# The fourth group of w_down by seven products, and the final norm in another order of columns

## The chip, the cores and the metric

One core of one Trainium2 chip. The metric is the device time of one execution in microseconds (us), lower is better; before the change it was 947.31 us, the median of three runs (946.19 to 949.31).

## The reference, cut to what matters

The kernel is one layer of an encoder on 512 tokens of width 1024, in fp32. The change touches only its end:

```python
hn = rmsnorm(h, norm_mlp)
h = h + square(relu(hn @ w_up)) @ w_down     # w_up 1024x4096, w_down 4096x1024
out = rmsnorm(h, norm_final)                 # rows scaled by (mean of squares + 1e-6)**-0.5
```

## The kernel before, in words

**Precision.** Each fp32 product is made of three fp32r matmuls. An operand `src` is split into a high part (a copy rounded to fp32r, on ACT, line 96) and a low part (`src` less the high part, on DVE, line 103). TensorE (PE) then adds high x high, low x high and high x low in PSUM.

**The stage w_up, w_down.** The 4096 hidden features go in four groups `g` of 1024. `up_unit(g, m)` makes 128 hidden features for all 512 tokens (24 matmuls of 512 columns, a relu and a square on ACT into `R[g, m // 4]`). Groups 0, 1 and 2 of w_down are multiplied in Strassen-Winograd form: hidden features and output columns are halved, tokens too, and seven products of a 256-token by 512-feature operand "A" with a 512x512 operand "B" take the place of eight. Each is 24 matmuls: `product(g, x)`, x from 0 to 6. The A operands are blocks of `R` or their sums `S1` to `S4` (`a_sum`, on DVE or POOL) and are split by `a_split`; the B operands are blocks of w_down or their sums `T1` to `T4` (`b_sum`, on POOL, 128x1024 each, T2, T3, T4 written over a block), two halves `q` each. Group 3 is multiplied plainly: `tokmajor` for output columns 0 to 511, then `tok_inner` for each of the four blocks `t` of 128 tokens for columns 512 to 1023, the last block in two halves of 256 columns.

**Sums.** A product ends in PSUM, and `add_to` adds it to `h_t` on DVE. The PSUM tile of products 2, 4 and 6 is one chain ("b"), that of 3 and 5 another ("c"). Product 0 of each group has a tile of its own and goes into an SBUF sum `X1` (`add_x1`); `x1_out` adds X1 to all eight parts of `h_t` on POOL during group 3.

**What sets the order.** It is written by hand. A tick is three matmuls; `later(n, f)` issues f n ticks on, and each engine works through its own instructions in the order of issue, as soon as what they read is there. `plan(g)` (line 1391) puts the sums and A splits of a group at ticks. The pieces of weights (and B halves) stand in one list; `use(i)` (line 235) issues the splits of piece i + 2, its high part one tick on, its low part two. Three buffers of each part go round (line 197), so that the split of a piece waits until the piece three before it has been multiplied. Between product x and x + 1 of a group stands `up_unit(g + 1, x)`, and two of them (6 and 7) end the group. A unit lasts eight ticks, as a product does, and uses one piece where a product uses two.

**The end.** The last norm takes blocks of 128 tokens in turn: squares of columns 0 to 511 early, then `add_h`, squares of the rest (ACT), a scale and a power of one column (POOL), and one `stt` of 128x1024 on DVE that writes `hn`, from which the block is stored. The last block's halves each end with an add (DVE) and squares (ACT), in PSUM tiles of their own:

```python
for q in range(2):
    p = ps()
    ...
    tt(h[:, hc], p[:, c], h[:, hc], ADD)
```

Of the kernel before, what the change touches and what calls it, by code (L numbers as in the profile page):

```python
# [9 lines left out]
F32 = mybir.dt.float32  # L10
# [8 lines left out]
L = 512  # L19
# [36 lines left out]
def trunk(ctx: ExitStack, tc: tile.TileContext, a: dict, out):  # L56
# [7 lines left out]
    def fr(t):  # L64
        return t.bitcast(F32)
# [14 lines left out]
    def zr():  # L80
        return z(F32R)
# [20 lines left out]
    def tt(o, i, j, op, eng=None):  # L102
        (eng or VE).tensor_tensor(out=o, in0=i, in1=j, op=op)  # L103
# [150 lines left out]
    def rows(w, k0, nk, c0, n=512):  # L254
        return w[k0 * 128:(k0 + nk) * 128, c0:c0 + n].rearrange("(k p) f -> p k f", p=128)
# [26 lines left out]
    DN = ("11", "21", "T2", "T1", "T3", "22", "T4")  # L282
    Bt = {}
    P_up = [[] for _ in range(4)]
    P_st, P_dn3 = [], [[], []]

    def add_up(g, m):
        P_up[g].append(add_piece(cols(w_up, 1024 * g + 128 * m)))

    for m in range(8):  # L290
        add_up(0, m)
    for g in range(3):
        P_st.append([])
        for x, nm in enumerate(DN):
            P_st[g].append([add_piece(lambda g=g, nm=nm, q=q: Bt[g, nm, q], "s") for q in range(2)])
            add_up(g + 1, x)
        add_up(g + 1, 7)
# [1037 lines left out]
    X1 = [mlp_p.tile([128, 512], F32, name=f"X{t}") for t in range(2)]  # L1335

    R, A_hl, S_t = {}, {}, {}
    T0, T1 = slice(0, 256), slice(256, 512)
# [14 lines left out]

    AN = ("A11", "A12", "S2", "S1", "S3", "S4", "A22")

    def a_split(g, x):
        def hi():
            src = a_block(g, x) if AN[x][0] == "A" else S_t[g, AN[x]]
            h = str_p.tile([128, 4, 256], F32R, tag="ah", name="ah", bufs=3)
            copy(SE, h, src)  # L1360
            A_hl[g, x] = (src, h)

        def lo():
            src, h = A_hl[g, x]
            l = str_p.tile([128, 4, 256], F32R, tag="al", name="al", bufs=3)
            tt(l, src, fr(h), SUB)
# [20 lines left out]
    def b_t1(g):  # L1387
        for q in range(2):
            later(4 * q, lambda q=q: b_sum(g, "T1", q, "12", "11", SUB))

    def plan(g):

        ra, rb = R[g, 0], R[g, 1]
        at = lambda n, *fs: [later(n + i, f) for i, f in enumerate(fs)]
        S = lambda nm: (lambda: S_t[g, nm])
        at(4, *a_split(g, 1))
        at(6, lambda: a_sum(g, "S1", lambda: ra[:, :, T1], lambda: rb[:, :, T1], ADD, VE))
        at(8, lambda: a_sum(g, "S2", S("S1"), lambda: ra[:, :, T0], SUB, VE))
        at(18, *a_split(g, 2))
        at(22, lambda: a_sum(g, "S4", lambda: rb[:, :, T0], S("S2"), SUB, GE))  # L1400
        for n, x in ((34, 3), (50, 4), (66, 5), (82, 6)):
            at(n, *a_split(g, x))
# [15 lines left out]
    def add_x1(g, t, p):
        if g == 0:
            copy(SE, X1[t], p)  # L1420
        else:
            tt(X1[t], p, X1[t], ADD)

    chain = {}

    CH = (("a", None), ("d", (0, 0)), ("b", (0, 1)), ("c", (1, 1)), ("b", (1, 1)), ("c", (0, 1)), ("b", (1, 0)))

    def product(g, x):
# [4 lines left out]
        acc = chain[g, nm]  # L1433
        for q in range(2):
            hs, ls = use(P_st[g][x][q])
            ah, al = A_hl[g, x]
            for i in range(2):
                k = 2 * q + i
                for t in range(2):
                    o = slice(128 * t, 128 * t + 128)  # L1440
                    st, sp = first and k == 0, k == 3
                    kw = {} if first else {"skip_group_check": True}
                    TE.matmul(acc[t], ah[:, k, o], hs[i], start=st, stop=False, **kw)  # L1443
                    TE.matmul(acc[t], al[:, k, o], hs[i], start=False, stop=False, **kw)  # L1444
                    TE.matmul(acc[t], ah[:, k, o], ls[i], start=False, stop=sp, **kw)  # L1445
                    tick()
        for t in range(2):
            if to is None:
                later(1 + t, lambda t=t: add_x1(g, t, acc[t]))
            else:  # L1450
                later(1 + t, lambda t=t: add_to(2 * to[0] + t, to[1], acc[t]))


    us = []
# [22 lines left out]
    aT_h, aT_l = [], []

    def a3(m):
        h, l = zr(), zr()  # L1480
        aT_h.append(h)
        aT_l.append(l)
        r = R[3, m // 4][:, m % 4]
        copy(SE, h, r)
        tt(l, r, fr(h), SUB)

    def x1_out(t, hf):
        o = h_t[t][:, 512 * hf:512 * hf + 512]
        tt(o, X1[t % 2], o, ADD, GE)

    for g in range(3):
        plan(g)
        for x in range(7):
            product(g, x)
            up_unit(g + 1, x)
        if g == 2:

            str_p.release()
            z_p = tc.alloc_tile_pool(name="z2", bufs=36, reuse_waits="tile")
            for m in range(4):  # L1500
                later(2 * m, lambda m=m: a3(m))
        up_unit(g + 1, 7)
    for m in range(4, 8):
        later(2 * m - 7, lambda m=m: a3(m))
    for n in range(8):
        later(2 + 2 * n, lambda n=n: x1_out(n // 2, n % 2))
    add_all(0, tokmajor(P_dn3[0], aT_h, aT_l))
    for t in range(3):
        p = tok_inner(P_dn3[1], aT_h, aT_l, t)
        o = hn_tile()  # L1510
        first_squares(t, o)
        add_h(t, 1, p)
        norm_rows(t, g_fin, o)
# [4 lines left out]
    first_squares(t, o)
    hg = xT_p.tile([128, 8, L], F32, tag="h", name="hg").rearrange("p a b -> p (a b)")[:, 0:1024]

    g32 = hg[:, 768:1024]
    ts(g32, g_fin[:, 768:1024], 32.0, 1.0, MUL, MUL, GE)
    stt(hg[:, 0:512], h[:, 0:512], 32.0, g_fin[:, 0:512], MUL, MUL)
    s2 = sm(2)
    for q in range(2):
        p = ps()
        c, hc = slice(256 * q, 256 * q + 256), slice(512 + 256 * q, 768 + 256 * q)
        for k in range(8):
            hs, ls = splits[P_dn3[1][k // 2]]
            mm3(p[:, c], aT_h[k][:, tok], aT_l[k][:, tok], hs[k % 2][:, c], ls[k % 2][:, c], k == 0, k == 7)  # L1530
        tt(h[:, hc], p[:, c], h[:, hc], ADD)
        SE.activation(out=o[:, hc], in_=h[:, hc], func=AF.Square, accum_out=s2[:, q:q + 1])
        if q == 0:
            tt(ss_t[t], ss_t[t], s2[:, 0:1], ADD, GE)
            stt(hg[:, hc], h[:, hc], 32.0, g_fin[:, hc], MUL, MUL)
    rs = sm()
    tt(rs, s2[:, 1:2], ss_t[t], ADD, GE)
    tt(rs, rs, mhalf, ALU.pow, GE)
    stt(o[:, 768:1024], h[:, 768:1024], rs, g32, MUL, MUL)
    SE.activation(out=o[:, 0:512], in_=hg[:, 0:512], func=AF.Copy, scale=rs)  # L1540
    SP.dma_start(out=out[tok, 768:1024], in_=o[:, 768:1024])
    SP.dma_start(out=out[tok, 0:512], in_=o[:, 0:512])
    ts(o[:, 512:768], hg[:, 512:768], rs, 1.0, MUL, MUL)
    SP.dma_start(out=out[tok, 512:768], in_=o[:, 512:768])
# [73 lines left out]
```

## Time and profile before

| | us |
|---|---|
| median of three runs | 947.31 |
| the profiled execution's own time | 945.39 |
| its span (first to last instruction) | 943.5 |
| PE busy | 920.4 |
| DVE busy | 589.6 |
| ACT busy | 446.3 |
| POOL busy | 342.7 |

All sections of the trace count from the start of the span. PE's records overlap each other, since matmuls are pipelined: the distance from one start to the next says what a matmul costs, not the length of its record. The low parts on DVE, the sums on POOL and the adds all have line 103, as they go through one helper; they are told apart by the names of their tiles.

### The profile page before, as it was taken

To read this page: it belongs to the slowest core of one execution; us is meant where nothing else is said; L and a number is where in the kernel's file an instruction comes from. 1 tells how busy PE (TensorE), PEld (TensorE's weight loads), DVE (VectorE), ACT (ScalarE), POOL (GpSimd) and SP (SyncE) were. 2 spreads that over 40 slices of the span, in tenths; PEclk is the share of its full clock that TensorE was granted. 3 is DMA by queue.
4 is the path that set the end of the run, shared out by engine and by line. 5 is a ranking of instruction groups with operands and counts; after the bars stand their busy time and mean duration, and the time that the engine had idled before them with its cause. 6 is when DMAs were issued, how large, how long until landed. Compare 5 with 4: busy or idle time off the path is not lost.

```text
span 943.5 us, 12801 instructions
## 1 busy us (share of the span) xinstructions
PE 920.4 (98%) x4683; PEld 739.0 (78%) x4683; DVE 589.6 (62%) x897; ACT 446.3 (47%) x711; POOL 342.7 (36%) x440
## 2 busy tenths in 40 slices
PE   9899989999999999998999999999999999999997
PEld 6788767777767888886888888888888888888876
DVE  4688778886653765668374554436665857775443
ACT  5634656656754334455343343346444444444522
POOL 0600246555788886233110000146134314511302
PEclk9999989999999999999999999999999999999998
DMA  9237666542312335354512255272333124221222
GB/s 315 87 116 197 166 166 178 167 136 85 103 48 78 90 90 138 82 139 130 159 47 89 90 170 186 68 250 62 94 112 130 49 94 148 90 67 45 67 90 90
DMA packets 140462, 111.05 MB, mean 118 GB/s; under 512 B 16368, under 2 KB 117104, under 8 KB 140400
## 3 DMA queue, kind: packets, MB, share of 16 engines
q1 hardware_dynamic: 140400, 110.24, 39.3%
q8 instruction: 37, 0.61, 0.3%
q14 instruction: 25, 0.20, 0.1%
HBM read 106.32 MB, written 3.90 MB: 117 GB/s over the span
## 4 chain that ended last, share of the span: by engine, by line
PE 87%; DVE 6%; ACT 2%; issue 2%; DMA 2%; POOL 1%; SPq 0%; POOLq 0%; DVEq 0%; ACTq 0%
PE ps L122 22%; PE ps L121 22%; PE ps L123 22%; PE ps L1444 4%; PE ps L1445 4%; PE ps L1443 4%; PE ps L810 3%; PE ps L794 2%; DVE z L103 1%; ACT z L96 1%; PE ps L1124 1%; PE ps L764 1%; PE ps L763 1%; DVE S L767 1%; DVE wl L103 1%
## 5 line engine op out<-in xcount | busy, mean ns | idle before, releaser
L103 DVE TENSOR_TENSOR wl<-raw,wh 128x1024 fp32r<-128x1024 f32 (+1 forms) x113 | 159.6, 1414 | 169.8 <-ACT wh L96 169.0
L121 PE MATMUL ps<-xh,wh 128*128 128x512 f32 x384 | 156.6, 408 | 0.0
L123 PE MATMUL ps<-xh,wl 128*128 128x512 f32 x384 | 150.7, 393 | 2.9 <-DVE wl L103 2.9
L122 PE MATMUL ps<-xl,wh 128*128 128x512 f32 x384 | 150.2, 391 | 0.0
L96 ACT ACTIVATE wh<-raw 128x1024 fp32r<-128x1024 f32 (+1 forms) x112 | 117.5, 1049 | 35.3 <-PE ps L123 7.9
L96 ACT ACTIVATE z<-ps 128x512 f32<-128x512 f32 (+4 forms) x128 | 72.9, 578 | 65.1 <-PE ps L123 24.2
L122 PE MATMUL ps<-hl,wh 128*128 128x512 f32 (+1 forms) x272 | 102.5, 377 | 0.3 <-DVE hl L103 0.3
L121 PE MATMUL ps<-hh,wh 128*128 128x512 f32 (+1 forms) x272 | 102.5, 377 | 0.2 <-ACT hh L96 0.2
L123 PE MATMUL ps<-hh,wl 128*128 128x512 f32 (+1 forms) x272 | 102.5, 377 | 0.0
L123 PEld LDWEIGHTS ps<-xh,wl 128*128 128x128 f32 x384 | 72.3, 188 | 19.1 <-DVE wl L103 3.3
L109 POOL TENSOR_SCALAR S<-S,sm 128x512 f32<-128x512 f32 x64 | 58.5, 930 | 79.1 <-DMA z<-Ud 58.7
L121 PEld LDWEIGHTS ps<-xh,wh 128*128 128x128 f32 x384 | 72.7, 189 | 14.2 <-PE ps L810 0.8
L122 PEld LDWEIGHTS ps<-xl,wh 128*128 128x128 f32 x384 | 72.8, 190 | 12.9
L1344 ACT ACTIVATE R<-ps 128x512 f32<-128x512 f32 x32 | 19.1, 598 | 128.2 <-PE ps L123 128.2
L103 POOL TENSOR_TENSOR z<-z 128x512 f32<-128x512 f32 x24 | 39.4, 1661 | 92.8 <-DVE z L106 42.2
L774 ACT ACTIVATE S<-S,sm 128x512 f32<-128x512 f32 x64 | 46.2, 722 | 56.1 <-DVE sm L109 52.7
L1443 PE MATMUL ps<-wh,ah 128*128 128x512 f32 x168 | 65.4, 389 | 0.0
L1444 PE MATMUL ps<-wh,al 128*128 128x512 f32 x168 | 65.4, 389 | 0.0
L1445 PE MATMUL ps<-wl,ah 128*128 128x512 f32 x168 | 65.4, 389 | 0.0
L109 POOL TENSOR_SCALAR sm<-sm 128x1 f32<-128x1 f32 (+1 forms) x16 | 3.6, 223 | 163.0 <-ACT hn L1314 137.7
L103 DVE TENSOR_TENSOR z<-z 128x512 f32<-128x512 f32 (+1 forms) x68 | 55.7, 824 | 10.5 <-ACT z L96 7.0
L103 POOL TENSOR_TENSOR B<-B,B 128x1024 f32<-128x1024 f32 x18 | 51.3, 2865 | 28.8 <-DVE wl L103 14.0
(209 smaller groups left out, 1931.3 us busy)
## 6 DMA issues: line engine op xcount, KB each, us to landing
raw<-in_w_in_dram SPq DMA_DIRECT2D x55, 512.0 KB
raw<-in_w_up_dram SPq DMA_DIRECT2D x32, 512.0 KB
B<-in_w_down_dram SPq DMA_DIRECT2D x24, 512.0 KB
T<-in_ttab_dram SPq DMA_DIRECT2D x16, 448.0 KB
z<-Fd SPq DMA_DIRECT2D x16, 256.0 KB
raw<-in_w_branch_attn_dram SPq DMA_DIRECT2D x8, 512.0 KB
raw<-in_w_out_dram SPq DMA_DIRECT2D x8, 512.0 KB
raw<-in_w_down_dram SPq DMA_DIRECT2D x8, 512.0 KB
```

The costliest lines, as they stand in the source:

```text
L96: SE.activation(out=o, in_=i, func=AF.Copy, scale=scale)
L103: (eng or VE).tensor_tensor(out=o, in0=i, in1=j, op=op)
L109: (eng or VE).tensor_scalar(out=o, in0=i, scalar1=s1, scalar2=s2, op0=op0, op1=op1)
L121: TE.matmul(o, wh, xh, start=first, stop=False)
L122: TE.matmul(o, wh, xl, start=False, stop=False)
L123: TE.matmul(o, wl, xh, start=False, stop=last)
L774: SE.activation(out=s, in_=s, func=AF.Exp, bias=nm, accum_out=den[h][:, t:t + 1])
L810: TE.matmul(p[64 * b:64 * b + 64], vt[kt][h // 8][:, c:c + 64], pts.pop((h, kt)), start=kt == 0, stop=kt == 3)
L1344: SE.activation(out=r, in_=p, func=AF.Relu)
L1443: TE.matmul(acc[t], ah[:, k, o], hs[i], start=st, stop=False, **kw)
L1444: TE.matmul(acc[t], al[:, k, o], hs[i], start=False, stop=False, **kw)
L1445: TE.matmul(acc[t], ah[:, k, o], ls[i], start=False, stop=sp, **kw)
```

## The change

Group 3 of w_down is multiplied by seven products as well. Product 0 starts chain "b", is added to block (0, 0) and goes on under product 2; `X1`, `add_x1`, `x1_out` and `a3` go. The pieces are listed in one order with the products, and in group 2 the units of group 3 stand earlier: after products 4 and 5 two each, and none after product 6. In group 3 nothing stands between the products; its plan has other ticks, and the low parts of its A operands 3 to 6 go to POOL. The last norm takes the left columns of blocks 2 and 3 last, and `end` is product 6 of group 3 with that norm: `one(q, i, t, c)` issues three matmuls into `acc[t][:, c]` and a tick. What follows the last add is as before, with left and right columns changed over.

```diff
-    for x in range(8):
-        i, hf = x // 2, x % 2
-        P_dn3[hf].append(add_piece(rows(w_down, 24 + 2 * i, 2, 512 * hf), "wz"[hf]))
+    ORDER = []
+    for g in range(4):
+        for x in range(7):
+            ORDER.append(("p", g, x))
+            if g < 2:
+                ORDER += [("u", g + 1, x)] + [("u", g + 1, 7)] * (x == 6)
+            elif g == 2:
+                ORDER += [("u", 3, m) for m in ((0,), (1,), (2,), (3,), (4, 5), (6, 7), ())[x]]
...
+        last = g == 3
+        at(0 if last else 4, *a_split(g, 1))
+        at(1 if last else 6, lambda: a_sum(g, "S1", lambda: ra[:, :, T1], lambda: rb[:, :, T1], ADD, VE))
+        at(2 if last else 8, lambda: a_sum(g, "S2", S("S1"), lambda: ra[:, :, T0], SUB, VE))
+        at(4 if last else 18, *a_split(g, 2))
+        at(5 if last else 22, lambda: a_sum(g, "S4", lambda: rb[:, :, T0], S("S2"), SUB, GE))
+        for n, x in (((12, 3), (19, 4), (27, 5), (35, 6)) if last else ((34, 3), (50, 4), (66, 5), (82, 6))):
+            at(n, *a_split(g, x, GE if last else None))
         for q in range(2):
+            if not last:
+                at(2 + 4 * q, lambda q=q: b_sum(g, "T3", q, "22", "12", SUB))
+            at((4 + 2 * q) if last else (12 + 4 * q), lambda q=q: b_sum(g, "T2", q, "T3", "11", ADD))
+            at((20 + 3 * q) if last else (36 + 4 * q), lambda q=q: b_sum(g, "T4", q, "21", "T2", SUB))
+        if g < 3:
+            e = 8 * (g == 2)
...
-    CH = (("a", None), ("d", (0, 0)), ("b", (0, 1)), ...
+    CH = (("b", (0, 0)), ("d", (0, 0)), ("b", (0, 1)), ...
...
+    def norm_out(t, c, scale, eps):
+        o = o_t[t]
+        s2 = sm()
+        SE.activation(out=o[:, c], in_=h_t[t][:, c], func=AF.Square, accum_out=s2)
+        rs = sm()
+        ts(s2, s2, ss_t[t], scale, ADD, MUL, GE)
+        tt(rs, s2, mhalf, ALU.pow, GE)
+        stt(o, h_t[t], rs, g_fin, MUL, MUL)
         SP.dma_start(out=out[t * 128:t * 128 + 128, :], in_=o)
...
+    def end(one, acc):
+        for q in range(2):
+            for i in range(2):
+                one(q, i, 0)
+        add_to(2, 0, acc[0])
+        norm_out(2, lo, 1.0 / D, EPS)
...
+        stt(hg[:, 512:1024], h[:, 512:1024], 32.0, g_fin[:, 512:1024], MUL, MUL)
+        for n in range(2):
+            c = slice(256 * n, 256 * n + 256)
+            for q in range(2):
+                for i in range(2):
+                    one(q, i, 1, c)
+            tt(h[:, c], acc[1][:, c], h[:, c], ADD)
+            SE.activation(out=o[:, c], in_=h[:, c], func=AF.Square, accum_out=s2[:, n:n + 1])
...
+        if g == 3 and x == 5:
+            for t in range(2):
+                later(3 + t, lambda t=t: norm_out(t, slice(512, 1024), 1.0 / D, EPS))
```

## Rows read from the trace of the kernel before

**Rows 1.** The page: busy time by engine, and the chain that ended last.
```profile
PE 920.4 (98%) x4683; PEld 739.0 (78%) x4683; DVE 589.6 (62%) x897; ACT 446.3 (47%) x711; POOL 342.7 (36%) x440
...
PE 87%; DVE 6%; ACT 2%; issue 2%; DMA 2%; POOL 1%; SPq 0%; POOLq 0%; DVEq 0%; ACTq 0%
```

**Rows 2.** Waits of PE, 560 to 945 us: waiting, releaser, us, times, longest.
```profile
PE ps L122 <- DVE wl L103: 1.4, 1, 1.4
```

**Rows 3.** Timeline of PE, 884 to 945 us: start, us, engine, line, operation, [idle].
```profile
890.80 0.39 PE L121 MATMUL ps<-wh,z 128*128 128x512 f32 x1
...
896.24 0.39 PE L121 MATMUL ps<-wh,z 128*128 128x512 f32 x1
898.07 0.50 PE L122 MATMUL ps<-wl,z 128*128 128x512 f32 x1 [1.44 <-DVE wl L103]
...
930.38 0.39 PE L123 MATMUL ps<-z 128*128 128x512 f32 x1
930.61 0.28 PE L121 MATMUL ps<-z 128*128 128x256 f32 x1
...
936.24 0.28 PE L123 MATMUL ps<-z 128*128 128x256 f32 x1
```

**Rows 4.** Groups by line and form, 560 to 945 us: busy us, mean ns.
```profile
L96 ACT ACTIVATE wh<-B 128x1024 fp32r<-128x1024 f32 x36 | 37.9, 1052 | 17.2 <-PE ps L1444 10.3 <-issue 5.8 <-POOL T L103 1.2
...
L103 DVE TENSOR_TENSOR h<-ps,h 128x512 f32<-128x512 f32 x51 | 33.1, 682 | 13.8 <-PE ps L123 13.8
...
L103 POOL TENSOR_TENSOR S<-R 128x1024 f32<-128x1024 f32 x3 | 7.2, 2401 | 77.6 <-ACT R L1345 55.1 <-DMA B<-in_w_down_dram 22.5
```

**Rows 5.** Timeline of POOL, 817 to 827 us.
```profile
817.56 2.40 POOL L103 TENSOR_TENSOR S<-R,S 128x1024 f32<-128x1024 f32 x1 [7.07 <-DVE S L103]
819.91 6.75 POOL L103 TENSOR_TENSOR B<-B,B 128x1024 f32<-128x1024 f32 x2
```

**Rows 6.** Timeline of DVE over the same stretch.
```profile
816.19 1.22 DVE L103 TENSOR_TENSOR S<-S,R 128x1024 f32<-128x1024 f32 x1
817.33 1.28 DVE L103 TENSOR_TENSOR X<-ps,X 128x512 f32<-128x512 f32 x2
818.53 2.51 DVE L103 TENSOR_TENSOR wl<-B,wh 128x1024 fp32r<-128x1024 f32 x1
822.53 1.87 DVE L103 TENSOR_TENSOR wl<-raw,wh 128x1024 fp32r<-128x1024 f32 x1 [1.49 <-ACT wh L96]
824.32 3.42 DVE L103 TENSOR_TENSOR al<-S,ah 128x1024 fp32r<-128x1024 f32 x1
```

**Rows 7.** Timeline of ACT after the last unit of group 3.
```profile
885.56 0.60 ACT L1344 ACTIVATE R<-ps 128x512 f32<-128x512 f32 x1 [7.33 <-PE ps L123]
886.19 0.63 ACT L1345 ACTIVATE R<-R 128x512 f32<-128x512 f32 x1
```

**Rows 8.** Timeline of PE, 40 to 49 us: before and after an idle stretch.
```profile
44.30 0.79 PE L122 MATMUL ps<-wl,z 128*128 128x512 f32 x1 [2.39 <-DVE wl L103]
...
45.32 0.63 PE L121 MATMUL ps<-wh,z 128*128 128x512 f32 x1
...
47.46 0.51 PE L123 MATMUL ps<-wh,z 128*128 128x512 f32 x1
47.80 0.39 PE L121 MATMUL ps<-wh,z 128*128 128x512 f32 x1
```

**Rows 9.** Timeline of DVE at the end.
```profile
930.81 0.69 DVE L103 TENSOR_TENSOR h<-ps,h 128x512 f32<-128x512 f32 x1 [1.61 <-PE ps L123]
933.36 1.28 DVE L106 SCALAR_TENSOR_TENSOR hn<-h,sm,g 128x1024 f32<-128x1024 f32 x1 [1.86 <-POOL sm L103]
934.56 0.88 DVE L106 SCALAR_TENSOR_TENSOR hg<-h,g 128x512 f32<-128x512 f32 x1
935.37 0.41 DVE L103 TENSOR_TENSOR h<-ps,h 128x256 f32<-128x256 f32 x1
...
936.56 0.42 DVE L103 TENSOR_TENSOR h<-ps,h 128x256 f32<-128x256 f32 x1 [0.32 <-PE ps L123]
```

More of the change, by code (lines that the diff above doesn't have):

```diff
@@ L284, in trunk @@
     P_up = [[] for _ in range(4)]
-    P_st, P_dn3 = [], [[], []]
+    P_st = [[] for _ in range(4)]
     def add_up(g, m):
         P_up[g].append(add_piece(cols(w_up, 1024 * g + 128 * m)))
+    ORDER = []
[6 more added lines that the diff above has]
+                ORDER += [("u", 3, m) for m in ((0,), (1,), (2,), (3,), (4, 5), (6, 7), ())[x]]
     for m in range(8):
         add_up(0, m)
-    for g in range(3):
-        P_st.append([])
-        for x, nm in enumerate(DN):
-            P_st[g].append([add_piece(lambda g=g, nm=nm, q=q: Bt[g, nm, q], "s") for q in range(2)])
-            add_up(g + 1, x)
-        add_up(g + 1, 7)
-    for x in range(8):
-        i, hf = x // 2, x % 2
-        P_dn3[hf].append(add_piece(rows(w_down, 24 + 2 * i, 2, 512 * hf), "wz"[hf]))
+    for kind, g, x in ORDER:
+        if kind == "u":
+            add_up(g, x)
+        else:
+            nm = DN[x]
+            P_st[g].append([add_piece(lambda g=g, nm=nm, q=q: Bt[g, nm, q], "s") for q in range(2)])
     ident = const.tile([128, 128], F32, name="ident")
@@ L1334, in trunk @@
     str_p = tc.alloc_tile_pool(name="strassen", bufs=1, reuse_waits="tile")
-    X1 = [mlp_p.tile([128, 512], F32, name=f"X{t}") for t in range(2)]
     R, A_hl, S_t = {}, {}, {}
@@ L1354, in trunk, with a_split @@
     AN = ("A11", "A12", "S2", "S1", "S3", "S4", "A22")
-    def a_split(g, x):
+    def a_split(g, x, eng=None):
         def hi():
@@ L1365, in lo @@
             l = str_p.tile([128, 4, 256], F32R, tag="al", name="al", bufs=3)
-            tt(l, src, fr(h), SUB)
+            tt(l, src, fr(h), SUB, eng)
             A_hl[g, x] = (h, l)
@@ L1395, in plan @@
         S = lambda nm: (lambda: S_t[g, nm])
[L1396 to L1402, printed above, removed]
-        for q in range(2):
-            at(2 + 4 * q, lambda q=q: b_sum(g, "T3", q, "22", "12", SUB))
-            at(12 + 4 * q, lambda q=q: b_sum(g, "T2", q, "T3", "11", ADD))
-            at(36 + 4 * q, lambda q=q: b_sum(g, "T4", q, "21", "T2", SUB))
@@ L1407, in plan @@
-        if g < 2:
+        last = g == 3
[6 more added lines that the diff above has]
+            at(n, *a_split(g, x, GE if last else None))
@@ L1408, in plan @@
+        for q in range(2):
+            if not last:
[4 more added lines that the diff above has]
+            e = 8 * (g == 2)
             for n, nm in ((44, "11"), (76, "12"), (92, "22"), (108, "21")):
                 at(n, lambda nm=nm: b_load(g + 1, nm))
-            at(112, lambda: b_t1(g + 1))
@@ L1411, in plan @@
-            at(98, lambda: a_sum(g + 1, "S3", lambda: R[g + 1, 0][:, :, T0], lambda: R[g + 1, 0][:, :, T1], SUB, GE))
-            at(104, *a_split(g + 1, 0))
+            at(112 - e, lambda: b_t1(g + 1))
+            if g == 2:
+                for q in range(2):
+                    at(113 + 3 * q, lambda q=q: b_sum(3, "T3", q, "22", "12", SUB))
+            at(98 - e, lambda: a_sum(g + 1, "S3", lambda: R[g + 1, 0][:, :, T0], lambda: R[g + 1, 0][:, :, T1], SUB, GE))
+            at(104 - e, *a_split(g + 1, 0))
@@ L1416, in add_to, with product @@
         tt(o, p, o, ADD)
[L1418 to L1422, printed above, removed]
     chain = {}
-    CH = (("a", None), ("d", (0, 0)), ("b", (0, 1)), ("c", (1, 1)), ("b", (1, 1)), ("c", (0, 1)), ("b", (1, 0)))
-    def product(g, x):
+    CH = (("b", (0, 0)), ("d", (0, 0)), ("b", (0, 1)), ("c", (1, 1)), ("b", (1, 1)), ("c", (0, 1)), ("b", (1, 0)))
+    def product(g, x, end=None):
         nm, to = CH[x]
@@ L1433, in product, with one @@
         acc = chain[g, nm]
+        def one(q, i, t, c=slice(0, 512), last=None):
+            hs, ls = splits[P_st[g][x][q]]
+            ah, al = A_hl[g, x]
+            k = 2 * q + i
+            o = slice(128 * t, 128 * t + 128)
+            st = first and k == 0
+            kw = {} if first else {"skip_group_check": True}
+            TE.matmul(acc[t][:, c], ah[:, k, o], hs[i][:, c], start=st, stop=False, **kw)
+            TE.matmul(acc[t][:, c], al[:, k, o], hs[i][:, c], start=False, stop=False, **kw)
+            TE.matmul(acc[t][:, c], ah[:, k, o], ls[i][:, c], start=False, stop=k == 3, **kw)
+            tick()
+        if end:
+            for q in range(2):
+                use(P_st[g][x][q])
+            end(one, acc)
+            return
         for q in range(2):
-            hs, ls = use(P_st[g][x][q])
-            ah, al = A_hl[g, x]
+            use(P_st[g][x][q])
             for i in range(2):
-                k = 2 * q + i
                 for t in range(2):
[L1440 to L1446, printed above, removed]
+                    one(q, i, t)
         for t in range(2):
[L1448 to L1451, printed above, removed]
+            later(1 + t, lambda t=t: add_to(2 * to[0] + t, to[1], acc[t]))
     us = []
@@ L1476, in trunk @@
         up_unit(0, m)
[L1477 to L1513, printed above, removed]
-        SP.dma_start(out=out[t * 128:t * 128 + 128, :], in_=o)
-    t, h, o = 3, h_t[3], hn_tile()
-    tok = slice(384, 512)
@@ L1518, in trunk @@
[L1518 to L1544, printed above, removed]
+    o_t = {}
+    def half_squares(t, hf):
+        o_t[t] = hn_tile() if t < 2 else raw()
+        ss_t[t] = sm()
+        c = slice(512 * hf, 512 * hf + 512)
+        SE.activation(out=o_t[t][:, c], in_=h_t[t][:, c], func=AF.Square, accum_out=ss_t[t])
@@ new lines, in norm_out, with ss_eps, early @@
+    def norm_out(t, c, scale, eps):
[6 more added lines that the diff above has]
+        stt(o, h_t[t], rs, g_fin, MUL, MUL)
+        SP.dma_start(out=out[t * 128:t * 128 + 128, :], in_=o)
+    def ss_eps(t):
+        ts(ss_t[t], ss_t[t], 1.0, D * EPS, MUL, ADD, GE)
+    def early(t, hf):
+        half_squares(t, hf)
+        ss_eps(t)
@@ new lines, in end @@
+    def end(one, acc):
+        lo = slice(0, 512)
+        for q in range(2):
+            for i in range(2):
+                one(q, i, 0)
+        add_to(2, 0, acc[0])
+        norm_out(2, lo, 1.0 / D, EPS)
+        h, o = h_t[3], o_t[3]
+        hg = xT_p.tile([128, 8, L], F32, tag="h", name="hg").rearrange("p a b -> p (a b)")[:, 0:1024]
+        g32 = hg[:, 256:512]
+        ts(g32, g_fin[:, 256:512], 32.0, 1.0, MUL, MUL, GE)
+        stt(hg[:, 512:1024], h[:, 512:1024], 32.0, g_fin[:, 512:1024], MUL, MUL)
+        s2 = sm(2)
+        for n in range(2):
+            c = slice(256 * n, 256 * n + 256)
+            for q in range(2):
+                for i in range(2):
+                    one(q, i, 1, c)
+            tt(h[:, c], acc[1][:, c], h[:, c], ADD)
+            SE.activation(out=o[:, c], in_=h[:, c], func=AF.Square, accum_out=s2[:, n:n + 1])
+            if n == 0:
+                tt(ss_t[3], ss_t[3], s2[:, 0:1], ADD, GE)
+                stt(hg[:, c], h[:, c], 32.0, g_fin[:, c], MUL, MUL)
+        rs = sm()
+        tt(rs, s2[:, 1:2], ss_t[3], ADD, GE)
+        tt(rs, rs, mhalf, ALU.pow, GE)
+        tok = slice(384, 512)
+        stt(o[:, 256:512], h[:, 256:512], rs, g32, MUL, MUL)
+        SE.activation(out=o[:, 512:1024], in_=hg[:, 512:1024], func=AF.Copy, scale=rs)
+        SP.dma_start(out=out[tok, 256:512], in_=o[:, 256:512])
+        SP.dma_start(out=out[tok, 512:1024], in_=o[:, 512:1024])
+        ts(o[:, 0:256], hg[:, 0:256], rs, 1.0, MUL, MUL)
+        SP.dma_start(out=out[tok, 0:256], in_=o[:, 0:256])
@@ new lines, in trunk @@
+    for kind, g, x in ORDER:
+        if kind == "u":
+            up_unit(g, x)
+            continue
+        if x == 0:
+            plan(g)
+        product(g, x, end if (g, x) == (3, 6) else None)
+        if g == 3 and x == 1:
+            for t in range(2):
+                later(4 + 2 * t, lambda t=t: early(t, 0))
+        if g == 3 and x == 4:
+            for t in range(2):
+                later(4 + t, lambda t=t: early(2 + t, 1))
+        if g == 3 and x == 5:
+            for t in range(2):
+                later(3 + t, lambda t=t: norm_out(t, slice(512, 1024), 1.0 / D, EPS))
@@ L1545, in trunk @@
+    str_p.release()
     h_p.release()
-    z_p.release()
     mlp_p.release()
```

## The prediction

> **What bounds the kernel now.** I read the page first: PE is busy for 98% of the span and makes 87% of the chain that ended last [rows 1]. So a microsecond is gained by taking matmuls away, as long as PE is not made to wait. Then the waits of PE for the end of the kernel: from 560 to 945 us only one exceeds 0.3, of 1.4 us, for a low part on DVE, in the plain multiplication of group 3 [rows 2, 3]. All else in the stage is hidden behind PE. Then PE's timeline for what a matmul costs. Between the starts 890.80 and 896.24 lie 24 steps, 0.2267 us each for 512 columns; the 48 matmuls of 256 columns from 930.61 to 936.24 take 0.12 us each [rows 3]. The records' own lengths (0.39) overlap and would say almost twice as much. A tick is thus 0.68 us and a product 5.44 us. Last I read DVE and POOL side by side where both are at work [rows 5, 6], since the change moves work to POOL and takes away the units between which DVE had time.
>
> What is to be seen there: the sum S4 on POOL takes 2.40 us from 817.56, undisturbed. The low part on DVE that starts at 818.53 takes 2.51 instead of 1.22, the time of a sum of its size at 816.19: it stands still until POOL ends at 819.96, and runs 1.08 from then. POOL's next pair takes 6.75 instead of 4.8, and DVE's two low parts beside it 1.87 and 3.42. All six instructions fit one rule, the two engines take turns by whole instructions: POOL holds for about 2.28 (from DVE's end at 824.39 to its own at 826.66), DVE for 1.08, and who comes second waits. Only the adds out of PSUM (X, two in 1.28) run through unhindered.
>
> **The change part by part.** I call G the moment when group 3's first matmul of w_down starts (890.80 now), and count from it. Up to G the amount of matmuls is the same; the order of units in group 2 changes, but nothing waits there now and each split still has 5.4 us, so 0 (at most the 1.4 us that the one wait cost).
>
> *Removed matmuls.* Now: 168 of 512 columns and 48 of 256, 38.1 + 5.8 = 43.9 us, and with the wait for DVE 45.6 (890.80 to 936.36). After: seven products of 24, the last one with 12 of its matmuls cut into 24 halves: 156 x 0.2267 + 24 x 0.12 = 38.2 us. The gain is 7.3 us: 5.6 of matmuls and 1.7 of the wait with its restart. X1's adds are replaced by as many adds to h (0), the eight `x1_out` on POOL and the splits of single hidden blocks go (hidden, 0), and eight loads of w_down become eight loads of the same 512 KB, issued on SP before G with nothing behind them but stores (0).
>
> *The feed of group 3.* A half product (2.72 us) needs one split: a high part on ACT, 1.05 [rows 4], and a low part on DVE, 1.22. It can start only when the piece three before is done, so 5.44 us before use. On DVE each product adds two adds of 0.68 [rows 4]; without POOL this is 3.8 us of 5.44 and fits. But POOL now has nine instructions of 2.40 in the same 33 us (T2 and T4 in two halves each, S4, four low parts of A), each holding DVE up for as much as 2.28. By hand, in DVE's order of issue:
> - The last unit ends at G-5.4; relu and square of it occupy ACT until G-4.1 [rows 7]; then come high and low part of product 0's two halves, until G-0.4. POOL's T2, first half, has waited for the second low part and holds until G+1.8.
> - DVE: an add (0.2), the low part of A12, which waits for POOL, G+1.8 to 2.9; S1 to 4.0; an add; S2 to 5.8; the low part of product 1's first half to G+6.9. PE wants it at G+5.9: it waits **1.1 us**.
> - S4 on POOL has waited since S2 and holds from G+6.9 to 9.2. The low part of S2 on DVE comes next, to 10.3; then T2's second half on POOL, to 12.6; then the low part of product 1's second half, to G+13.7. PE wants it at 9.8: **3.9 us**.
> - The clock: after an idle of 2.39 us PE went on at 0.43 us a matmul, the level of 1.2 GHz, for eight matmuls or so, 44.30 to 47.80 [rows 8], while an idle of 1.44 left it at 0.23 [rows 3]. The wait of 3.9 should do the same: eight times 0.2 and the restarts, **2.0 us**.
> - After that PE is late enough that DVE and POOL, in turns, keep ahead of it.
>
> Sum: product 6 starts at G + 32.66 (144 matmuls) + 7.0 = G+39.6. The low end of this term is 0, if DVE and POOL do not hinder each other there; the high end takes one more hold of 2.28 with its clock, 10.5.
>
> *The end.* Now the last 48 halves (5.8 us) cover the norm of block 2. After the change, DVE has in its queue behind product 5: the low part of the last piece, two adds, two `stt` of blocks 0 and 1, the add of block 2, its `stt`, the `stt` for hg, and only then the two adds of the last halves. Each `stt` of 1.28 waits for squares on ACT and two small steps on POOL: from the start of an add to the start of its `stt` 2.55 us (930.81 to 933.36), and what stands behind waits too [rows 9]. From product 6's start: the first add at 1.8, `stt` at 4.3 and 5.5, add of block 2 at 6.7, its `stt` at 9.2, hg at 10.4 (0.8), first half's add 11.2 to 11.6. PE has finished the first half at 4.2.
> The second half of the matmuls now goes to the other columns of the tile that this add reads; before, each half had a tile of its own, and ran through at 0.12 [rows 3]. No row shows one part of a PSUM tile read while another is written. I bound it by 0 (PE runs on at once; the second add then follows the hg `stt` at 12.0) and by a full wait: PE starts at 11.7 after 7 idle us, 12 halves at the slow level [rows 8], 0.24 each, and the second add starts at 14.9. I take the wait, as a write after a read of the same tile, and keep 2.9 us less for the range.
> The Trainium skill ("PSUM — Partial Sum Buffer", section "PSUM bank collisions raise a hardware error") says that TensorE writing and VectorE reading one bank and quadrant raise an error even at disjoint columns, and that PSUM is to be guarded by bank, not by address. By that rule the wait must be there; no run here shows it yet.
> From the second add to the span's end it is 943.5 - 936.56 = 6.94, unchanged: same steps, columns changed over.
>
> *Sum.* Now G to the second add: 45.8. After: 39.6 + 14.9 = 54.5. So +8.8 us, against the profiled execution's 945.39 (span 943.5 and 1.9 around it), which is 954.2. The median of the runs lies 1.9 above that execution, so for it 947.3 + 8.8 = **956.1 us**.
>
> **The rivals.**
> *No wait for the shared PSUM tile.* Only the end differs: the second add at 12.0, so +5.9 and 953.2. For it: the columns are disjoint. Against it: the tile is one.
> *DVE and POOL do not hinder each other* (the other side). Then group 3 has no wait and product 6 starts at G+32.7. The crowded end stays, as it waits for small steps and not for a shared resource: 10 to 12.6 us to the second add (the first add no longer stands behind a late low part, and starts at -0.5 instead of 1.8). That gives -3.3 without the tile's wait, 944.0, and -0.5 with it, 946.9. It decides by whether the low part of product 1's second half ends by G+9.8. For it: DVE and POOL each have less than 5.44 us a product on their own numbers. Against it: all the instructions of [rows 5, 6] but X.
> *Group 3 waits more than the hand chain says.* Low parts of 3.4 us as at 824.32 [rows 6] for products 3 to 5 exceed the 2.72 of a half; if one more wait goes to PE with its clock, +3.5: 959.6.
> That the change does not save the matmuls can be left out: their count follows from the code.
>
> **How the numbers follow.** The forecast (both the turns and the tile's wait) 0.50, no tile wait 0.22, no hindrance 0.14 (half of it on each of its two times), more waits 0.14. The range leaves out the no-hindrance case and little more: 949 to 960, where the low end leaves room for a feed that costs 3 us less than worked out. About 0.3% (2.8 us) is what a measurement of this kernel can tell from no change. Faster by more than that: 944.0 lies on the edge, so 0.08; within it 0.09; slower 0.83.
>
> **What would show it.** PE's waits in group 3 for `wl` and `al` on DVE line 103, the longest near product 1's second half; DVE records of `wl` and `al` of 2.2 to 3.5 us there beside POOL records of 3.4; matmuls at 0.43 after the longest wait; at the end three `stt` of 1.28 between the adds, and the second twelve halves starting just behind the first half's add, at 0.24. Wrong it is if PE's starts in group 3 lie 0.23 apart throughout, if DVE's low parts stay at 1.22 while POOL works, or if the 24 halves run through.

## The result, and the profile after

The changed kernel takes 955.68 us (median of four runs, 955.03 to 956.80) where the kernel before, run beside it, takes 946.75 (945.42 to 949.31). The ratio is 1.0077, with a 95% interval of 1.0053 to 1.0101: slower by 0.8%, some 7.3 us, between 5.0 and 9.6. (The two medians lie 8.9 apart, which is inside the interval.) The forecast was 956.1, +8.8. The profiled execution took 955.08 us, its span 953.3.

The page of after, busy time and chain [rows 1]: PE has 36 matmul records fewer and is busy for 2.4 us less, yet its share of the span falls from 98% to 96%. DVE gains 35 us of busy time and POOL 35, though POOL has only six instructions more. (The share of PE in the chain isn't compared: the chain is followed back to other waits than before.)

```profile
PE 918.0 (96%) x4647; PEld 735.3 (77%) x4647; DVE 624.6 (66%) x904; ACT 454.0 (48%) x710; POOL 377.6 (40%) x446
```

Where it stands is in the waits of PE in the span's last 390 us [rows 2]. The one wait of 1.4 us is gone; three others, one at the end and two in group 3, are there instead.

```profile
PE ps L1447 <- DVE h L103: 6.1, 1, 6.1
PE ps L1449 <- DVE wl L103: 4.5, 2, 3.6
```

PE's timeline of after [rows 3, 8] gives the marks. G, the start of group 3's first w_down matmul, is at 894.01. The low part of a piece is late twice, for 0.93 and 3.58 us. After the second wait matmuls start 0.43 apart for a while, and are back at 0.23 at 910.95. The twelve matmuls from 936.06 are the half product that is cut in halves; half a product (2.72) earlier, at 933.34, product 6 starts, which I call T. The second twelve halves start only at 943.80, 0.21 apart.

```profile
894.01 0.39 PE L1447 MATMUL ps<-wh,ah 128*128 128x512 f32 x1
...
900.99 0.50 PE L1449 MATMUL ps<-wl,ah 128*128 128x512 f32 x1 [0.93 <-DVE wl L103]
...
907.62 0.80 PE L1449 MATMUL ps<-wl,ah 128*128 128x512 f32 x1 [3.58 <-DVE wl L103]
908.21 0.63 PE L1447 MATMUL ps<-wh,ah 128*128 128x512 f32 x1
908.64 0.63 PE L1448 MATMUL ps<-wh,al 128*128 128x512 f32 x1
...
910.72 0.40 PE L1447 MATMUL ps<-wh,ah 128*128 128x512 f32 x1
910.95 0.40 PE L1448 MATMUL ps<-wh,al 128*128 128x512 f32 x1
...
936.06 0.28 PE L1447 MATMUL ps<-wh,ah 128*128 128x256 f32 x1
...
943.80 0.58 PE L1447 MATMUL ps<-wh,ah 128*128 128x256 f32 x1 [6.15 <-DVE h L103]
944.18 0.42 PE L1448 MATMUL ps<-wh,al 128*128 128x256 f32 x1
...
946.32 0.41 PE L1449 MATMUL ps<-wl,ah 128*128 128x256 f32 x1
```

Both waits in group 3 end with a low part on DVE. Here are DVE's and then POOL's records of that stretch [rows 5, 6]: the low parts take 3.30 and 3.35 us, not 1.21, each beside a POOL record of 3.33; the adds out of PSUM (`h<-ps,h`, two in 1.28) run at full speed beside POOL's 3.35.

```profile
899.72 1.21 DVE L103 TENSOR_TENSOR wl<-B,wh 128x1024 fp32r<-128x1024 f32 x1
900.98 3.30 DVE L103 TENSOR_TENSOR al<-S,ah 128x1024 fp32r<-128x1024 f32 x1
904.21 3.35 DVE L103 TENSOR_TENSOR wl<-B,wh 128x1024 fp32r<-128x1024 f32 x1
907.49 1.28 DVE L103 TENSOR_TENSOR h<-ps,h 128x512 f32<-128x512 f32 x2
```
```profile
899.88 3.33 POOL L103 TENSOR_TENSOR S<-R,S 128x1024 f32<-128x1024 f32 x1 [4.04 <-DVE S L103]
903.16 3.33 POOL L103 TENSOR_TENSOR B<-B,B 128x1024 f32<-128x1024 f32 x1
906.45 3.35 POOL L103 TENSOR_TENSOR al<-S,ah 128x1024 fp32r<-128x1024 f32 x1
```

DVE at the end [rows 9]: between product 5's adds and the first half's add (943.34) stand three `stt` of 128x1024, the add of block 2 and the `stt` for hg. PE restarts 0.05 us after that add's end; the second add is at 946.77.

```profile
930.15 3.36 DVE L103 TENSOR_TENSOR wl<-B,wh 128x1024 fp32r<-128x1024 f32 x2
933.43 1.28 DVE L103 TENSOR_TENSOR h<-ps,h 128x512 f32<-128x512 f32 x2
935.98 1.29 DVE L106 SCALAR_TENSOR_TENSOR hn<-h,sm,g 128x1024 f32<-128x1024 f32 x1 [1.27 <-POOL sm L103]
937.72 1.28 DVE L106 SCALAR_TENSOR_TENSOR hn<-h,sm,g 128x1024 f32<-128x1024 f32 x1 [0.44 <-POOL sm L103]
938.92 0.68 DVE L103 TENSOR_TENSOR h<-ps,h 128x512 f32<-128x512 f32 x1
941.39 1.42 DVE L106 SCALAR_TENSOR_TENSOR raw<-h,sm,g 128x1024 f32<-128x1024 f32 x1 [1.79 <-POOL sm L103]
942.74 0.68 DVE L106 SCALAR_TENSOR_TENSOR hg<-h,g 128x512 f32<-128x512 f32 x1
943.34 0.41 DVE L103 TENSOR_TENSOR h<-ps,h 128x256 f32<-128x256 f32 x1
...
946.77 0.42 DVE L103 TENSOR_TENSOR h<-ps,h 128x256 f32<-128x256 f32 x1 [2.56 <-PE ps L1449]
```

So G to the second add takes 52.76 us (before 45.76), of which 39.33 up to T and 13.43 behind it; from the second add to the span's end it is 6.53 (before 6.94). That is +6.6. The spans differ by 9.8: the other 3.2 lie ahead of G (894.01 against 890.80), and nearly all of it is there long before the w_up stage. POOL's first instruction of the last RMS norm before w_up, first of before, then of after:

```profile
577.41 0.19 POOL L109 TENSOR_SCALAR sm<-sm 128x1 f32<-128x1 f32 x1 [96.76 <-ACT hn L1314]
```
```profile
580.34 0.19 POOL L109 TENSOR_SCALAR sm<-sm 128x1 f32<-128x1 f32 x1 [96.38 <-ACT hn L1320]
```

Up to there the two programs issue the same instructions on every engine, so I take this difference as one between two executions; where it arises isn't shown. +6.6 from the marks fits the ratio's +7.3; the difference of the spans would have said too much. Below, kernels are compared by their marks (G, T, second add, end) and by the ratio to before.

### The profile page after: what moved, and what is told of

It reads as the page before. It is cut to its first block, busy times and chain, and to the rows that moved or that the text cites. A ratio compares the mean times of both kernels' runs of the same rounds, so it can differ in the third digit from the quotient of the medians.

```text
span 953.3 us, 12773 instructions
## 1 busy us (share of the span) xinstructions
PE 918.0 (96%) x4647; PEld 735.3 (77%) x4647; DVE 624.6 (66%) x904; ACT 454.0 (48%) x710; POOL 377.6 (40%) x446
## 4 chain that ended last, share of the span: by engine, by line
PE 76%; DVE 10%; DMA 4%; issue 3%; ACT 2%; SPq 2%; POOL 2%; POOLq 0%; DVEq 0%; ACTq 0%
PE ps L122 18%; PE ps L123 18%; PE ps L121 18%; PE ps L1449 5%; PE ps L1447 5%; PE ps L1448 5%; PE ps L816 3%; DVE wl L103 2%; DVE z L103 2%; PE ps L800 2%; DVE S L773 1%; DMA raw<-in_w_in_dram 1%; ACT z L96 1%; DVE xl L106 1%; DMA z<-in_s_bq_im_dram 1%
## 5 line engine op out<-in xcount | busy, mean ns | idle before, releaser
L96 ACT ACTIVATE wh<-raw 128x1024 fp32r<-128x1024 f32 (+1 forms) x108 | 113.2, 1049 | 30.1 <-PE ps L123 9.3
L1447 PE MATMUL ps<-wh,ah 128*128 128x512 f32 (+1 forms) x228 | 89.1, 391 | 6.1 <-DVE h L103 6.1
L1449 PE MATMUL ps<-wl,ah 128*128 128x512 f32 (+1 forms) x228 | 89.3, 392 | 4.5 <-DVE wl L103 4.5
L1448 PE MATMUL ps<-wh,al 128*128 128x512 f32 (+1 forms) x228 | 89.0, 390 | 0.0
L103 POOL TENSOR_TENSOR B<-B,B 128x1024 f32<-128x1024 f32 x24 | 71.5, 2992 | 43.6 <-DVE wl L103 27.0
L103 DVE TENSOR_TENSOR wl<-B,wh 128x1024 fp32r<-128x1024 f32 x48 | 73.0, 1526 | 15.0 <-ACT wh L96 14.8
```

Source lines behind the costliest of these rows:

```text
L96: SE.activation(out=o, in_=i, func=AF.Copy, scale=scale)
L1447: TE.matmul(acc[t][:, c], ah[:, k, o], hs[i][:, c], start=st, stop=False, **kw)
L1448: TE.matmul(acc[t][:, c], al[:, k, o], hs[i][:, c], start=False, stop=False, **kw)
L1449: TE.matmul(acc[t][:, c], ah[:, k, o], ls[i][:, c], start=False, stop=k == 3, **kw)
```

## The experiments

Theory: two losses outweigh 7.3 us of removed matmuls and wait. In group 3 POOL's wide instructions and DVE's block each other, so that low parts come late (6.7 us). At the end PE waits with its last twelve halves for a read of the same PSUM tile, and that read stands at the back of DVE's queue. Rivals: the tile's wait costs nothing by itself; DVE is simply overbooked; the new chain of sums costs something.

The times in us, each in a profiled execution of its kernel:

| kernel | ratio to before [95%] | G to T | T to second add | G to second add | from there to the end |
|---|---|---|---|---|---|
| before | 1 | | | 45.76 | 6.94 |
| after | 1.0077 [1.0053, 1.0101] | 39.33 | 13.43 | 52.76 | 6.53 |
| e1 own tile | 1.0052 [1.0033, 1.0071] | 39.42 | 11.03 | 50.45 | 6.55 |
| e2 no POOL | 0.9993 [0.9979, 1.0007] | 32.64 | 12.89 | 45.53 | 6.86 |
| e3 chain only | 0.9990 [0.9976, 1.0003] | | | 45.77 | 6.52 |
| e4 end's order | 1.0019 [1.0004, 1.0034] | 39.39 | 7.22 | 46.61 | 7.28 |
| e5 feed | 1.0004 [0.9990, 1.0018] | 33.32 | 14.12 | 47.44 | 6.50 |
| e6 all | 0.9941 [0.9923, 0.9960] | 33.27 | 7.77 | 41.04 | 7.45 |
| e7 end and tile | 1.0027 [1.0012, 1.0041] | 39.35 | 7.52 | 46.87 | 7.46 |
| e8 low parts on DVE | 1.0058 [1.0039, 1.0077] | 39.09 | 12.91 | 52.00 | 6.48 |
| e9 sums early | 1.0036 [1.0022, 1.0050] | 35.01 | 14.88 | 49.89 | 6.51 |

Each mark comes from one execution. How well such a mark repeats is to be seen in G to T of the four kernels with the same feed (after, e1, e4, e7): it lies between 39.33 and 39.42.

**e1, the second half in a PSUM tile of its own.**

```diff
+            own = ps() if n == 1 else None
-                    one(q, i, 1, c)
+                    one(q, i, 1, c, own)
-            tt(h[:, c], acc[1][:, c], h[:, c], ADD)
+            tt(h[:, c], (acc[1] if own is None else own)[:, c], h[:, c], ADD)
...
+            later(6, lambda: tt(h_t[3][:, c1], chain[3, "b"][1][:, c1], h_t[3][:, c1], ADD))
```

> The changed kernel, but the second half of the last twelve matmuls goes into a PSUM tile of its own (what stood in the right columns of the chain's tile is added to h earlier, by one more add of 128x256 on DVE during product 5). Theory (PE waits for the first half's add because both halves share a tile): the 24 halves run through at 0.12 us, the idle of 6.2 us at 937.4 goes, and the second add starts about 10.8 us after product 6's start instead of 13.4: 2.6 us less. Group 3's start to product 6's start stays at 39.3. Rival (PE waits there for something else on DVE, for instance the low part or the chain as a whole): the idle stays and so does the 13.4.

The 24 halves run through (PE's timeline), and the wait is gone; the second add now follows the first at once (DVE's).

```profile
938.55 0.28 PE L1450 MATMUL ps<-wl,ah 128*128 128x256 f32 x1
938.67 0.28 PE L1448 MATMUL ps<-wh,ah 128*128 128x256 f32 x1
```
```profile
944.76 0.41 DVE L103 TENSOR_TENSOR h<-ps,h 128x256 f32<-128x256 f32 x1
945.21 0.42 DVE L106 SCALAR_TENSOR_TENSOR hg<-h,g 128x256 f32<-128x256 f32 x1
945.55 0.42 DVE L103 TENSOR_TENSOR h<-ps,h 128x256 f32<-128x256 f32 x1
```

The tile's wait costs 2.4 us by the marks (11.03 where 10.8 was expected), near the 2.9 forecast less the added early add (0.41). It isn't 6.1, since DVE comes to the first half's add no sooner: PE idles under DVE's queue. (The intervals of the two ratios overlap, so that here the marks alone tell e1 from after.)

**e2, POOL's nine wide instructions of group 3 left out** (T3, another block of w_down and S2 stand in for T2, T4 and S4, and one low part serves four operands).

```diff
+        if g == 3 and nm in ("T2", "T4"):
+            Bt[g, nm, q] = Bt[g, i, q]
+            return
...
+        if (g, nm) == (3, "S4"):
+            S_t[g, nm] = S_t[g, "S2"]
+            return
...
+            if eng is GE:
+                A_hl[g, x] = (h, A_hl[3, 2][1])
+                return
```

> The changed kernel without POOL's nine 128x1024 instructions in group 3: T2, T4 and S4 are left out (T3, B21 and S2 stand in their places) and the low part of S2 serves A operands 3 to 6 too. DVE, ACT and PE have the same instructions as before. Theory (DVE's low parts are held up by POOL in turns): group 3's start to product 6's start falls from 39.3 to about 33, no wait of PE over 1 us there, DVE's low parts at 1.22, no 0.43 matmuls; 6 us less. Rival (eight products in a row starve on DVE's own load and order of issue or on the three buffers): the waits near product 1 stay, 3 us or more of the 5.5.

G to T is 32.64, the bare matmuls (144 x 0.2267 = 32.64). DVE executes the same list at full speed; the rows answer to those at 900.98, 904.21 and 907.49 of after:

```profile
898.31 1.23 DVE L103 TENSOR_TENSOR al<-S,ah 128x1024 fp32r<-128x1024 f32 x1
899.45 1.22 DVE L103 TENSOR_TENSOR wl<-B,wh 128x1024 fp32r<-128x1024 f32 x1
900.59 1.28 DVE L103 TENSOR_TENSOR h<-ps,h 128x512 f32<-128x512 f32 x2
```

All 6.7 us of the feed are POOL's doing. DVE's own list fits. The two low parts read nothing that POOL writes (S2 is made on DVE, block 21 is loaded), so it isn't that they waited for POOL's results: their records are longer.

**e3, the first product's sum in chain "b" alone, in the kernel before.** X1 and its eight adds on POOL go, group 3 stays plain.

```diff
-    CH = (("a", None), ("d", (0, 0)), ("b", (0, 1)), ...
+    CH = (("b", (0, 0)), ("d", (0, 0)), ("b", (0, 1)), ...
-    for n in range(8):
-        later(2 + 2 * n, lambda n=n: x1_out(n // 2, n % 2))
```

> The kernel before with one part of the change alone: product 0 starts chain b, is added to block (0, 0) and goes on under product 2; X1, its adds and x1_out go; group 3 stays plain. Theory (this part costs and gains nothing, PE has the same matmuls and no wait there): group 3's start to the second add stays at 45.8, same time within 0.3%. Rival (POOL's eight x1_out had hindered the low parts of group 3's feed): the wait of 1.4 us in group 3 shrinks and up to 1.7 us are gained.

45.77 from G to the second add against 45.76: this part of the change costs nothing and gains nothing.

**e4, DVE's queue at the end in another order.** hg's right half before product 5's adds; the `stt` of block 1 behind the first half's add, that of block 2 behind the second's.

```diff
+            later(7, hg_right)
+            later(7, hg_32)
...
+        norm_fin(0)
-        norm_out(2, lo, 1.0 / D, EPS)
+        norm_pre(2, lo, 1.0 / D, EPS)
-        stt(hg[:, 512:1024], h[:, 512:1024], 32.0, g_fin[:, 512:1024], MUL, MUL)
...
+                norm_fin(1)
...
+        norm_fin(2)
```

> The changed kernel with another order of DVE's queue at the end: hg's right half and g32 right after product 4's adds; the add of block 2 behind the first stt only; the stt of block 1 behind the first half's add, the stt of block 2 behind the second half's. Both halves still share a tile. Theory (the end is bound by DVE's queue, in which each stt waits for small steps of other engines): the second add starts 6.6 us after product 6's start instead of 13.4, PE idles under 1.2 us, no matmul at 0.21: 6.8 us less. Rival (the end is bound by the shared tile, whatever the order): at most the 2.6 us of that wait are gained.

T to the second add falls from 13.43 to 7.22 (6.6 was expected). The tile is still shared, but the wait for it is 1.18 us, and after so short an idle PE goes on at 0.12 per half:

```profile
938.79 0.39 PE L1447 MATMUL ps<-wh,ah 128*128 128x256 f32 x1 [1.18 <-DVE h L103]
939.01 0.28 PE L1448 MATMUL ps<-wh,al 128*128 128x256 f32 x1
939.13 0.28 PE L1449 MATMUL ps<-wl,ah 128*128 128x256 f32 x1
```

Block 2's `stt` now comes last, behind the second add, and the way from that add to the end is 0.75 us longer; POOL's one-column add beside this `stt` takes 0.90 and not 0.19. The net gain is 5.4 (46.61 + 7.28 against 52.76 + 6.53); the order of the queue was the larger part of the end's loss.

**e7, e4 and e1's tile together** (e1's and e4's edits).

> The changed kernel with DVE's queue at the end in the other order and the second half of the last product in a PSUM tile of its own; group 3's sums as in the change. Theory (the wait for the shared tile and the queue ahead of the adds are one loss: the tile's wait is as long as the queue makes it): after the reorder only 1.2 us of that wait was left, so the own tile gains 0.5 to 1.2 us more, less an early add of 0.4 beside it; the second half's add 6.3 to 7.2 us after product 6's start, 45.6 to 46.6 from the first w_down matmul; about 949 to 950, same as before. Rival (the tile's wait is a cost by itself): it gains 2.3 us as it did in the kernel with the old queue, and ends near 947.5.

46.87, nothing gained over e4's 46.61: once the queue is right, the tile's wait no longer costs anything, and the early add takes DVE's time (7.52 behind T, above the 7.2 expected; 951.20 in all, above the 949 to 950 expected). The wait is as dear as the queue in front of the read.

**e5, group 3's sums in another order, all of them made.** T2, S1 and S2 late in group 2 (T2 into buffers of its own), S4 and T4 later, the four low parts on DVE.

```diff
-            at(n, *a_split(g, x, GE if last else None))
+            at(n, *a_split(g, x))
-        at(5 if last else 22, lambda: a_sum(g, "S4", ...
+        at(14 if last else 22, lambda: a_sum(g, "S4", ...
-            at((20 + 3 * q) if last else (36 + 4 * q), ...
+            at((24 + 6 * q) if last else (36 + 4 * q), ...
+        if g == 2:
+            at(114, lambda: a_sum(3, "S1", ...
+            at(115, lambda: a_sum(3, "S2", ...
+            for q in range(2):
+                at(117 + q, lambda q=q: b_sum(3, "T2", q, "T3", "11", ADD))
```

> The changed kernel with another order of group 3's sums, and the same sums: T2, S1 and S2 are made late in group 2, when the operands are there and PE still multiplies group 2's last products; S4 and T4 stand later in group 3; the low parts of A operands 3 to 6 are back on DVE. The end is untouched. Theory (POOL's wide instructions and DVE's block each other in turns, and early in group 3 that makes PE wait): with five wide POOL instructions fewer at that place, product 6 starts 33 to 34.5 us after group 3's first w_down matmul instead of 39.3, the second half's add follows 13 us later as before, 46.5 in all, and the time falls by 5 to 6.5 us to about 949. Rival (group 3 is short of DVE time itself, and leaving POOL out helped only because sums were left out with it): all sums are made here, so PE's waits for low parts come back in another place, group 3 keeps 3 us or more of them, and the time stays above 952.

G to T is 33.32, with one wait of 0.3 us. All sums are made and the loss is nearly gone, so DVE isn't short of time in the whole. But two things were changed at once, the place of the sums and the engine of the four low parts; e8 and e9 take them apart. The end took 14.12, 0.7 more than in after, so G to the second add is 47.44 and not the 46.5 expected: the first add is at T+0.77 here (T+0.09 in after), and all behind it follows.

**e8 and e9, the two halves of e5's edit.** In e8 only the low parts go back to DVE; in e9 only the sums move and the low parts stay on POOL.

> The changed kernel with one edit: the low parts of group 3's A operands 3 to 6 go on DVE again, not on POOL; T2, S4 and T4 stay on POOL at their places. Theory (the stall comes from the three POOL sums that fall between the first four pieces' low parts: T2 in halves and S4): the waits of about 0.9 and 3.6 us near product 1 stay as they are, since the first low part on POOL begins only at the end of the second wait; product 6 starts 38.5 to 41 us after group 3's first w_down matmul (39.3 in the changed kernel), and the time is 954 to 957. Rival (it is the amount of POOL's work in the whole group, of which these four are nearly half): the waits shrink by half or more, product 6 starts by 36.5, and the time is 953 or less.

> The changed kernel with T2, S1 and S2 of group 3 made late in group 2, S4 and T4 later in group 3, and the low parts of A operands 3 to 6 left on POOL. Theory (place decides: the sums among the first four pieces): both waits near product 1 go, and product 6 starts 33 to 35 us after group 3's first w_down matmul, where the four low parts on POOL may cost one wait of up to 1.5 us later on; 949 to 951.5 in all. Rival (amount decides): with four of POOL's wide instructions still beside DVE's low parts, the waits move later and half or more of them is left, 36.5 us or more to product 6, and 952.5 or more in all.

Waits of PE in e8, and then in e9:

```profile
PE ps L1449 <- DVE wl L103: 4.5, 2, 3.6
```
```profile
PE ps L1460 <- DVE wl L103: 0.9, 3, 0.3
```

e8 leaves both waits as they were (39.09), against the rival's 36.5 or less. e9 takes them away and has three of 0.3 later, beside POOL's later wide instructions; with their restarts they make most of the 2.4 above the bare 32.64 (35.01, at the edge of what was expected; in the whole it is 0.5 us above it, as its first add is at T+1.54). Moving the sums gains 4.3 us, the low parts behind them another 1.7; the low parts alone gain 0.24. The stall is made by T2 and S4 among the first pieces. (e9 takes S1 and S2 out of DVE's queue there too; but e2 leaves them in place and has no wait. T4 starts at 916.58 in after, behind both waits.)

**e6, all three amendments** (e5's, e4's and e1's edits).

> The changed kernel with three amendments together, no work left out: group 3's sums in the other order, DVE's queue at the end in the other order, and the second half of the last product in a PSUM tile of its own. Theory (the seven products' gain is real, and was given back by the feed and by the end's queue alone): first w_down matmul of group 3 to product 6 33 to 34 us, from there to the second half's add 6.5 to 7, 40 in all against 45.8 before; 5 to 6 us faster than the kernel before, some 941 to 942. Rival (the two losses share a cause, or a next wait takes over at the end, such as the squares and stores of the early blocks that now all fall into the last 6 us): over 43 from the first matmul to the second half's add, or more than 8 us from that add to the end, and the time within 0.3% of before.

942.71 us (940.81 to 945.42) against 948.79 for before in the same job, ratio 0.9941 [0.9923, 0.9960]: 5.6 us faster than before, and about 13 faster than the change as made. Every sum is computed. The 942.71 is 0.7 above the 941 to 942 expected. PE's waits above 0.25 us in the last 390 us are down to two of 0.3:

```profile
PE ps L122 <- DVE hl L103: 0.3, 1, 0.3
PE ps L1461 <- DVE wl L103: 0.3, 1, 0.3
```

The marks give -4.2 (41.04 + 7.45 against 45.76 + 6.94), inside the interval. The 41.04 is one more than expected: the reordered DVE queue comes to the second add at T+7.77, while PE is done with product 6 at T+5.6. What is left of the loss is in DVE's queue, where `stt` of 128x1024 still stand ahead of the last add and the first of them waits 1.28 for POOL's small steps. DVE's timeline of e6:

```profile
929.85 1.29 DVE L106 SCALAR_TENSOR_TENSOR hn<-h,sm,g 128x1024 f32<-128x1024 f32 x1 [1.28 <-POOL sm L103]
...
932.46 1.28 DVE L106 SCALAR_TENSOR_TENSOR hn<-h,sm,g 128x1024 f32<-128x1024 f32 x1
933.65 0.42 DVE L103 TENSOR_TENSOR h<-ps,h 128x256 f32<-128x256 f32 x1
```

## Why the prediction was right, step by step

The direction, the two causes and their places were right. The size was about 1.5 us too big by the ratio and 2.2 by the marks (+8.8 against +7.3 and +6.6). That the median comes within 0.4 us of 956.1 is partly luck: the four runs of before beside it lie at 946.75, and in the later jobs its medians were 948.4 to 948.8.

| step | forecast | measured |
|---|---|---|
| matmuls from G to T, bare | 32.66 | 32.64 (e2) |
| first wait | 1.1 | 0.93 |
| second wait | 3.9 | 3.58 |
| clock and restarts | 2.0 | 2.2 |
| G to T | 39.6 | 39.33 |
| first add behind T | 1.8 | 0.09 |
| second `stt` | 5.5 | 4.38 |
| first half's add | 11.2 | 10.00 |
| second twelve halves start | 11.7 | 10.46 |
| second add | 14.9 | 13.43 |
| from there to the end | 6.94 | 6.53 |

*Removed matmuls.* Right: 32.64 for 144 of them in e2. That they are a gain in time takes e6 to see.

*The feed.* The hand chain in turns of 2.28 and 1.08 said that the late low part ends at G+13.7; it ended at 904.21 + 3.35, G+13.55. 2.28 + 1.08 is 3.36, and the records beside each other last 3.30 to 3.35 on both engines. The Trainium skill states the rule in "SBUF — State Buffer", section "Who interferes with whom": a DVE instruction with two SBUF inputs contends with a GpSimd (POOL) instruction that reads SBUF, one with at most one SBUF input doesn't outside the 2-port modes, and the ports that the two engines share are an exclusive lock. The rows agree: the adds, with one input in PSUM, keep 1.28 for two, the low parts don't keep 1.21.

*The clock.* After 3.58 idle, 907.62 to 910.95 are eight steps in 3.33 us, where at 0.2267 they take 1.81: 1.5 us. The other 0.65 are mostly the two restarts. The granted clock was 0.65 over 907.6 to 912; the halves at the end, after 6.15 idle, ran at 0.50, which is the 1.2 GHz level. After 1.18 in e4 there was no fall, nor after 0.93. But the row I went by [rows 8], a fall after 2.39 idle, is less than a rule: the same matmul of after, at 44.16 after 2.37 idle, goes on at 0.23 (granted clock 1.00 over 44.16 to 47.70, against 0.52 in before). Another matmul, the same in both kernels, does it the other way round, first before, then after:

```profile
441.27 0.50 PE L123 MATMUL ps<-xh,wl 128*128 128x512 f32 x1 [2.92 <-DVE wl L103]
```
```profile
443.30 0.80 PE L123 MATMUL ps<-xh,wl 128*128 128x512 f32 x1 [2.91 <-DVE wl L103]
```

The granted clock is 1.00 over 441.27 to 444.60 and 0.53 over 443.30 to 446.60. So idles of 2.4 to 2.9 us were followed by either level. After the 3.6 of group 3 it fell in all five kernels that have this wait, in e1 and e7 only some 0.6 us after PE had restarted. The 2.0 was right; the row behind it was one of two outcomes.

*The end: the term that was mis-sized.* I put the first add at T+1.8, behind a late low part. DVE had the last two low parts done at 933.51, T+0.17, so all of it began 1.7 us earlier. Half a microsecond was lost again, because the second `stt` came 1.74 behind the first and not 1.2 (below); some 0.3 was gained by the slow halves, 0.21 apart and not 0.24. The result, 13.43, is 1.5 under the forecast.

*The tile.* The full wait was right, and "no tile wait" is out: PE waited 6.15 us for the read of other columns, and with a tile of its own it didn't (e1). That agrees with the rule I had from the Trainium skill, "PSUM — Partial Sum Buffer", section "PSUM bank collisions raise a hardware error", to guard PSUM by bank and not by address; but the wait is one that the program's semaphores make, and what happens without it wasn't tried.

*The rival of the other side* (no hindrance, 944.0 or 946.9) described e2 well: 45.53 from G with the tile's wait, -0.2 against before where I had -0.5. It was the right price for a condition that doesn't hold in the change.

*The rival of more waits* (959.6) didn't come: behind 910.95 and up to T the longest step of PE is 0.34, at 927.99.

## What to carry to other kernels

Work moved to an idle engine is priced by what it does to its neighbour: find one pair of overlapping records in the trace, take the hold of each from it, and go through the queue by hand. Then ask where the moved work falls: with the sums among the first pieces the feed lost 6.7 us, with the same sums made before or after them 2.4, and with the low parts back on DVE as well 0.7. A wait for a shared buffer is as dear as the queue ahead of the read that frees it; put that read in front before giving it a buffer of its own.

## What was not expected

Instructions of a single column on POOL are held up as well. POOL's timeline at the end of after: the power takes 0.56 us with DVE idle, and 1.39 beside the `stt` of 935.98; it ends 0.41 behind that `stt`, and the second `stt` waits for it.

```profile
935.39 0.56 POOL L103 TENSOR_TENSOR sm<-sm,mhalf 128x1 f32<-128x1 f32 x1
...
936.29 1.39 POOL L103 TENSOR_TENSOR sm<-sm,mhalf 128x1 f32<-128x1 f32 x1
```

The effect of place is not additive with that of amount, as far as one execution of each kernel shows: taking four of POOL's nine instructions away gains 0.24 us with the sums at their old place, and 1.7 with the sums moved.
